# First stage of a three-block model: convolution taps moved from TensorE to ScalarE and GpSimd, level products summed before use, states in two PSUM banks

## The chip, the cores and the metric

The kernel runs on one core of a Trainium2 chip. The time is the device time of one execution in microseconds (us), and less is better. The engines are named as the profile names them: PE (TensorE), PEld (its weight loads), DVE (VectorE), ACT (ScalarE), POOL (GpSimd) and SP (SyncE, which only issues DMAs). SBUF is the on-chip working memory, PSUM the eight banks that PE writes its sums to.

## The reference, cut to what matters

A sequence of 256 tokens with 1024 features passes through a model of a first block with two layers and a second block. Each layer of the first block is a mixer and a product-key expert layer. Only the mixer of the first layer, `even_mix`, is touched:

```
p = h @ w_in                                  # h: rms-normed x
a_val, a_gate, q, k, v, r, glr = split(p)
# branch a, 512 channels: gate, causal depthwise convolution of 31 taps, layer norm, silu
u = a_val * sigmoid(a_gate)
y_a = silu(layer_norm(conv31(u) + conv_b))
# branch b, 4 heads of 64/128: gated linear attention in chunks of 64 tokens
log_a = log_sigmoid(glr @ gate_w2 + gate_b) / 16
attn[t,s] = sum_k q[t,k] k[s,k] exp(b[t,k] - b[s,k])   # b: cumulative log_a in the chunk, s <= t
o = (q exp(b)) @ state + attn @ v;  state = state*exp(b_last) + (k exp(b_last-b))^T @ v
y_b = rms_norm(o) * silu(r)
x = x + concat(y_a, y_b) @ w_out
```

The kernel computes the decayed attention of 128 tokens without dividing by small exponentials: it writes the causal triangle as seven "levels" (half widths 32, 16, 8, 4, 2, 1 and the diagonal). At each level the products of suitably scaled keys and queries are right on some blocks, which a 0/1 mask keeps; the sum over the levels is `attn`.

## The kernel before, in words

**Tiling.** Features lie on the 128 partitions, the 256 tokens on the free dimension. Weights arrive as a stream of blocks of 128x1024 in float32 (`Stream`, w_raw). ACT rounds each block to w_hi (L337), DVE subtracts for w_lo (L353), and a projection (`proj_t`) takes 24 PE passes: 8 slices of the features, each as hi*hi, hi*lo and lo*hi. A plain float32 product takes two PE passes instead. Blocks marked plain (row blocks 0 to 5) are used as float32 without the split.

**The first stage, in the order in which PE gets it** (`even`, L638): the values v (`natural`, 4 blocks), the small gate projection glr (`decays`), branch c=0 (aval, agate), keys and queries (kq, 4), branches c=1 to 3 (aval, agate), the output gates r (4), the rest of the eight chains, and the eight row blocks of w_out in the order 4, 5, 6, 7, 0, 1, 2, 3 (`Rows`). Row blocks 4 to 7 need the attention output (two heads each), 0 to 3 the convolution branch after its layer norm.

**What sets the order of the small work.** Every engine works through its instructions in program order, and the order is written by hand with two devices. `flow` is a list of generators: each call of `flow.step()` advances every one of them to its next `yield`. `bg` holds the convolution steps of DVE: `bg.run(slack)` issues steps until their nominal cost has used up the slack. `tick(n, slack)` (L900) adds the next chain if the levels are done, steps `flow` once and runs `bg`. There is one tick after each projection (slack 1200, three convolution steps), two after each r (2000, five steps each), one for each further chain, and one in each turn of the loop over the row blocks (2500). Evacuations of a projection are issued after the next projection (`lagged`, `flush`), those of r at once. The loop over the row blocks adds `layer_norm` when `bg` is empty, and a row block when its inputs are in the set `ready`.

**The convolution.** For each group c of 128 channels, `gated` writes ub, the gated input with 30 zero columns ahead. Taps 0 to 7 are done by PE (`conv_pe`, L775): POOL has made 8 diagonal matrices dg from the identity and the taps (`taps`, L656), and 8 float32 products, 16 passes, sum ub shifted by the tap into bank 7; ACT copies the sum to yp. Taps 8 to 30 are 23 steps on DVE into yc (`conv`, L765 and L769). `layer_norm` starts with yc += yp (L862), then mu_b, centring, squares, var, square root, rs_b, scaling and silu.

**The attention.** `decays` makes the scaled keys and queries z of the levels. `states` (L787) makes the three states, each in one PSUM bank taken from the list `pa`, which holds only bank 3 at this point. `inner` (L811) is a chain for one head and 128 tokens, eight in all. In its first tick it makes seven products pm, 14 passes, on 64 partitions, in banks 2 and 6; in the second DVE masks them into sm (L822, L823); in the third PE adds all seven sm times the values, and the states' share, into oT:

```
for l in range(7):
    mm(oT[p][...], vn[:, tb, hd * P:(hd + 1) * P], sm[:, l], p not in started, l == 6)
```

After chain 4 and chain 8 `head_norm` follows in three ticks: squares; o_ps and a square root; ob, two products and, for row blocks 6 and 7, a split (`parts`, which also marks the row blocks ready).

Of the kernel before, what the change touches and what calls it, by code (L numbers as in the profile page):

```python
# [20 lines left out]
P = 128  # L21
S = 256
# [19 lines left out]
EV_ROWS = (4, 5, 6, 7, 0, 1, 2, 3)  # L42
CONV_PE = 8
U_SLACK = 1300
# [334 lines left out]
def body(ctx: ExitStack, tc: tile.TileContext, a, out, phases=(0, 6)):  # L379
# [6 lines left out]
    class Banks:  # L386
# [5 lines left out]
        def set(self, banks):  # L392
            self.banks, self.i = banks, 0
# [16 lines left out]
    def acc(i, name="acc"):  # L410
        return psum.tile([P, 512], F32, tag=f"bank{4 + i}", name=f"{name}{i}")
# [15 lines left out]
    def col(name, i=0, n=1):  # L427
        at, w = COLS[name]
        assert i + n <= w
        return cols[:, at + i:at + i + n]  # L430
# [207 lines left out]
    def even():  # L638
        banks((0, 1), (2, 3))
        with even_pool as es:  # L640
# [7 lines left out]
            tri64, = masks(sp, 3, 4)  # L648
            dgs = deque()

            def taps():
                c = len(dgs) + pe_done
                if c < 4:
                    dg = tp.tile([P, CONV_PE, P], F32, name="dg", tag="dg")
                    for j in range(CONV_PE):
                        nc.gpsimd.tensor_scalar(dg[:, j], ident, col("convw", c * CONVW + j), None, op0=OP.mult)  # L656
                    dgs.append(dg)

            f2 = lambda t: t.rearrange("p a b -> p (a b)")
# [5 lines left out]
            def parts(k0, n):  # L665
                for k in range(k0, k0 + n):
                    if k in split_k:
                        i = split_k.index(k)
                        split_to(y[0][:, i], y[1][:, i], yf[:, k])
                    ready.add(k)  # L670

# [17 lines left out]
            def decays():  # L689
# [7 lines left out]
                proj_small(h, gws, ps[:16, :S], 16)  # L697
                while norm["steps"] is not None:
                    yield
# [64 lines left out]
            def conv(c):  # L764
                nc.vector.tensor_scalar(yc[:, c], ub[:, c, CONV_PE:CONV_PE + S], col("convw", c * CONVW + CONV_PE),  # L765
                                        col("convb", c), op0=OP.mult, op1=OP.add)
                yield 300
                for j in range(CONV_PE + 1, CONVW):
                    nc.vector.scalar_tensor_tensor(yc[:, c], ub[:, c, j:j + S], col("convw", c * CONVW + j),  # L769
                                                   yc[:, c], op0=OP.mult, op1=OP.add)  # L770
                    yield 400

            pe_done = 0

            def conv_pe(c):  # L775

                nonlocal pe_done
                pe = acc(3, "pe")
                dg = dgs.popleft()
                for j in range(CONV_PE):  # L780
                    mm(pe[:, :S], dg[:, j], ub[:, c, j:j + S], j == 0, j == CONV_PE - 1)
                yield
                nc.scalar.activation(yp[:, c], pe[:, :S], AF.Copy)
                pe_done += 1
                taps()

# [24 lines left out]
            def inner(hd, tb):  # L811
# [8 lines left out]
                yield  # L820
                sm = tp.tile([P, 7, P], F32, name="sm", tag="sm", bufs=2)
                nc.vector.tensor_mul(f2(sm[:, :4]), pm[0], f2(lmask[:, :4]))  # L822
                nc.vector.tensor_mul(f2(sm[:, 4:]), pm[1][:, :3 * P], f2(lmask[:, 4:]))  # L823
                yield
                if not oT:
                    oT.extend(psum.tile([P, 512], F32, tag=f"bank{i}", name="oT") for i in range(2))
                for l in range(7):
                    mm(oT[p][:, e * S + tb * P:e * S + (tb + 1) * P], vn[:, tb, hd * P:(hd + 1) * P], sm[:, l],
                       p not in started, l == 6)
                    started.add(p)  # L830
                for c in (2 * tb, 2 * tb + 1):
# [57 lines left out]

            ready = set()  # L890
            chains = deque(inner(2 * p + e, tb) for p in range(2) for tb in range(2) for e in range(2))
# [8 lines left out]
            def tick(n, slack):  # L900
                for _ in range(n):
                    if "levels" in done:
                        if "states" not in done:
                            done.add("states")
                            flow.add(states())
                        elif chains:
                            flow.add(chain(chains.popleft()))
                    flow.step()
                    bg.run(slack)
# [5 lines left out]
            for j in range(4):  # L915
                natural(va, j)
                if j == 1:
                    flow.add(decays())
                if j >= 2:
                    taps()  # L920
                flow.step()
# [7 lines left out]
            def branch(c):  # L929
# [7 lines left out]
                def gated():  # L937
# [5 lines left out]
                    bg.add(conv(c))  # L943
                    flow.add(conv_pe(c))

# [6 lines left out]
            for t, scale in ((kT, 1.0), (qT, 0.125)):  # L952
                for p in range(2):
# [3 lines left out]
                    tick(1, E_SLACK)  # L957
            banks((4, 5), (3,))
            flush()
# [13 lines left out]
            while len(chains) > E_LATE:  # L973
                tick(1, E_SLACK2)
            pm_banks[1] = 3
            rows = Rows(y, [split_k.index(k) if k in split_k else k for k in EV_ROWS], yf)
            while rows.n < 6:
# [870 lines left out]
```

## Time and profile before

| | us |
|---|---|
| time, median of 3 runs (lowest, highest) | 2348.55 (2344.61, 2349.74) |
| the profiled execution | 2352.38 |
| its span in the profile | 2350.6 |
| first row block of the stage begins (PE) | 138.41 |
| row block 0 begins (PE) | 161.52 |

Of the span PE is busy 99%, PEld 97%, DVE 73%, ACT 58% and POOL 4%. A busy PE isn't PE at its peak: its clock is granted at one of two levels, 1.2 and 2.4 GHz, and the column PEclk gives the mean of a stretch as a share of the upper one. "Busy" counts the time in which an engine has an instruction at work; a wait row names who ended an engine's idle time. The first stage ends, with the last row block, at about 175 us of the span; then the expert layer of the first layer begins, whose code isn't touched, nor is any later stage.

### The profile page before, as it was taken

How to read it: one execution, taken by the hardware profiler on the slowest of the kernel's cores; microseconds unless marked ns; L12 is line 12 of the kernel's file. 1: busy time of each engine (PE TensorE's matmuls, PEld its weight loads, DVE VectorE, ACT ScalarE, POOL GpSimd, SP SyncE). 2: the span in 40 equal slices, each digit the busy share in tenths (PEclk: the TensorE clock that was granted, in tenths of full speed). 3: DMA queues.
4: the chain of work that ended last, by engine and by line, in shares of the span. 5: the costliest groups of instructions: out<-in, count | busy, mean ns of one | idle time of the engine just before them, and what ended most of it. 6: DMA issues, size and time to landing. Idle time of an engine off the chain costs nothing. (4 is left out here: it accounts for less than half of the span.)

```text
span 2350.6 us, 48812 instructions
## 1 busy us (share of the span) xinstructions
PE 2315.8 (99%) x19664; PEld 2268.3 (97%) x19664; DVE 1723.3 (73%) x3656; ACT 1357.8 (58%) x2480; POOL 93.6 (4%) x107
## 2 busy tenths in 40 slices
PE   8999999999999999999999999999999999999999
PEld 7889999999999999998899999999999999999999
DVE  6668999999755555566699899996555555667983
ACT  6226448888544444455564588884444445555762
POOL 4100000000000000010000000000000000002300
PEclk9899999999999999999999999999999999999999
DMA  6114654444555666553256544446556565645553
GB/s 214 54 63 163 193 185 156 149 145 140 174 185 185 206 186 184 178 193 117 89 165 190 186 145 147 144 142 188 185 185 206 185 185 161 210 137 177 181 182 123
DMA packets 106626, 386.82 MB, mean 165 GB/s; under 512 B 11959, under 2 KB 13272, under 8 KB 106016
## 3 DMA queue, kind: packets, MB, share of 16 engines
q1 hardware_dynamic: 104976, 377.99, 50.7%
q0 software_dynamic: 1136, 5.32, 0.7%
q8 instruction: 154, 2.52, 0.4%
q14 instruction: 72, 0.59, 0.1%
q10 hardware_dynamic: 288, 0.40, 0.1%
HBM read 383.40 MB, written 1.05 MB: 164 GB/s over the span
## 5 line engine op out<-in xcount | busy, mean ns | idle before, releaser
L353 DVE TENSOR_TENSOR w_lo<-w_raw,w_hi 128x1024 fp32r<-128x1024 f32 x710 | 866.4, 1224 | 383.9 <-ACT w_hi L337 382.3
L337 ACT ACTIVATE w_hi<-w_raw 128x1024 fp32r<-128x1024 f32 x710 | 745.6, 1054 | 432.6 <-PE pv L452 348.0
L452 PE MATMUL pu<-h_hi,w_hi 128*128 128x256 f32 x2048 | 586.9, 287 | 0.0
L452 PE MATMUL pu<-h_lo,w_hi 128*128 128x256 f32 x2048 | 575.2, 281 | 0.0
L452 PE MATMUL pu<-h_hi,w_lo 128*128 128x256 f32 x2048 | 574.5, 281 | 0.0
L452 PE MATMUL pv<-h_hi,w_hi 128*128 128x256 f32 x1888 | 530.4, 281 | 0.0
L452 PE MATMUL pv<-h_lo,w_hi 128*128 128x256 f32 x1888 | 530.4, 281 | 0.0
L452 PE MATMUL pv<-h_hi,w_lo 128*128 128x256 f32 x1888 | 530.4, 281 | 0.0
L452 PEld LDWEIGHTS pu<-h_lo,w_hi 128*128 128x128 f32 x2048 | 386.4, 189 | 0.0
L452 PEld LDWEIGHTS pu<-h_hi,w_lo 128*128 128x128 f32 x2048 | 385.8, 188 | 0.0
L452 PEld LDWEIGHTS pu<-h_hi,w_hi 128*128 128x128 f32 x2048 | 385.5, 188 | 0.0
L452 PEld LDWEIGHTS pv<-h_hi,w_lo 128*128 128x128 f32 x1888 | 355.8, 188 | 0.0
L452 PEld LDWEIGHTS pv<-h_lo,w_hi 128*128 128x128 f32 x1888 | 355.8, 188 | 0.0
L452 PEld LDWEIGHTS pv<-h_hi,w_hi 128*128 128x128 f32 x1888 | 355.8, 188 | 0.0
L1271 ACT ACTIVATE X<-pu 128x256 f32<-128x256 f32 (+31 forms) x228 | 74.1, 325 | 197.2 <-PE pu L452 197.1
L1168 ACT ACTIVATE oa<-cb,routed 128x128 bf16<-128x128 f32 x512 | 162.9, 398 | 0.0
L1173 DVE TENSOR_TENSOR ob<-ob,g 128x512 bf16<-128x512 bf16 x256 | 108.0, 422 | 4.4
L452 PEld LDWEIGHTS <-oa 128*128 128x128 bf16 x1536 | 90.2, 96 | 12.9 <-issue 5.3
L452 PE MATMUL g<-ob,oa 128*128 128x128 bf16 x1024 | 102.1, 219 | 0.0
L452 PE MATMUL g<-oa 128*128 128x128 bf16 x512 | 94.7, 219 | 0.3
L461 DVE TENSOR_TENSOR h_lo<-X,h_hi 128x512 fp32r<-128x512 f32 (+1 forms) x134 | 86.4, 653 | 2.1 <-ACT h_hi L460 1.9
L1174 ACT ACTIVATE oa<-oa 128x512 bf16<-128x512 bf16 x128 | 80.8, 631 | 4.1
(450 smaller groups left out, 4122.3 us busy)
## 6 DMA issues: line engine op xcount, KB each, us to landing
w_raw<-in_s_u SPq DMA_DIRECT2D x256, 512.0 KB, 3.6
w_raw<-in_s_v SPq DMA_DIRECT2D x256, 512.0 KB, 3.6
w_raw<-in_s_mix SPq DMA_DIRECT2D x46, 512.0 KB, 3.9
w_raw<-in_s_up SPq DMA_DIRECT2D x44, 512.0 KB, 4.3
w_raw<-in_s_wq SPq DMA_DIRECT2D x32, 512.0 KB, 3.7
w_raw<-in_s_odd SPq DMA_DIRECT2D x32, 512.0 KB, 4.0
w_raw<-in_s_even SPq DMA_DIRECT2D x28, 512.0 KB, 3.9
w_raw<-in_s_down SPq DMA_DIRECT2D x22, 512.0 KB, 4.2
```

The source lines that it names most:

```text
L337: self.nc.scalar.activation(hi, raw, AF.Copy)
L353: self.nc.vector.tensor_sub(lo, raw, hi.bitcast(F32))
L452: nc.tensor.matmul(o, l, r, start=start, stop=stop, skip_group_check=True)
L461: nc.vector.tensor_sub(lo, src, hi.bitcast(F32))
L1168: nc.scalar.activation(o[0][:, i * P:(i + 1) * P], iota, AF.Abs, bias=ne1T[:, t0 + i:t0 + i + 1])
L1173: nc.vector.tensor_tensor(two[part], two[2], pairs(g3[:, part, t0:t0 + GT]), op=OP.mult)
L1174: nc.scalar.activation(o[0], o[0], AF.Relu, bias=1.0, scale=-1.0)
L1271: nc.scalar.activation(X(c)[:, td:], ps[:, td:S], AF.Gelu)
```

## The change

Five things are changed, all in `even`.

1. `conv_pe`, the diagonal matrices and their maker `taps` go. `conv_pool(c)` takes their place in `flow`: for each of taps 0 to 7 ACT writes ub shifted, times the tap, to a tile (tap 0 straight to yp, taps 1 to 7 to one of four tiles), and POOL adds the tile to yp. It does two taps per tick, so it takes four ticks for a group.
2. In `inner` POOL sums the seven masked levels in four adds (three levels to three, then 2 += 6, 0 += 1, 0 += 2), and PE then makes one float32 product with the values in place of seven. The chain has one more tick between masks and product, and sm has three buffers instead of two.
3. After kq the list `pa` holds banks 3 and 7 (bank 7 is free, as PE's convolution is gone) until the chains are all begun; then bank 3 alone.
4. `decays` begins after the first value block instead of the second, so that the split of the small gate weights and the glr products come one block earlier; it then waits until the sum of squares is complete.
5. `parts` marks row blocks in `late`, and `tick` moves them to `ready` at its start, so a row block is released one tick later.

The core of the diff:

```diff
-            dgs = deque()
-            def taps():
-                ...
-                    ready.add(k)
+                    late.add(k)
...
-                while norm["steps"] is not None:
+                while norm["steps"] is not None or norm["n"] < KD:
                     yield
...
-            def conv_pe(c):
-                pe = acc(3, "pe")
-                dg = dgs.popleft()
-                for j in range(CONV_PE):
-                    mm(pe[:, :S], dg[:, j], ub[:, c, j:j + S], j == 0, j == CONV_PE - 1)
-                yield
-                nc.scalar.activation(yp[:, c], pe[:, :S], AF.Copy)
-                ...
+            def conv_pool(c):
+                for j in range(CONV_POOL):
+                    t = tp.tile([P, S], F32, name="tap", tag="tap", bufs=4) if j else yp[:, c]
+                    nc.scalar.activation(t, ub[:, c, j:j + S], AF.Copy, scale=col("convw", c * CONVW + j))
+                    if j:
+                        nc.gpsimd.tensor_tensor(yp[:, c], yp[:, c], t, op=OP.add)
+                    if j % 2:
+                        yield
...
-                sm = tp.tile([P, 7, P], F32, name="sm", tag="sm", bufs=2)
+                sm = tp.tile([P, 7, P], F32, name="sm", tag="sm", bufs=3)
                 nc.vector.tensor_mul(f2(sm[:, :4]), pm[0], f2(lmask[:, :4]))
                 nc.vector.tensor_mul(f2(sm[:, 4:]), pm[1][:, :3 * P], f2(lmask[:, 4:]))
+                add = lambda o, a_, b_: nc.gpsimd.tensor_tensor(o, a_, b_, op=OP.add)
+                add(f2(sm[:, 0:3]), f2(sm[:, 0:3]), f2(sm[:, 3:6]))
+                add(sm[:, 2], sm[:, 2], sm[:, 6])
+                add(sm[:, 0], sm[:, 0], sm[:, 1])
+                add(sm[:, 0], sm[:, 0], sm[:, 2])
+                yield
                 yield
                 ...
-                for l in range(7):
-                    mm(oT[p][:, e * S + tb * P:e * S + (tb + 1) * P], vn[:, tb, hd * P:(hd + 1) * P], sm[:, l],
-                       p not in started, l == 6)
-                    started.add(p)
+                mm(oT[p][:, e * S + tb * P:e * S + (tb + 1) * P], vn[:, tb, hd * P:(hd + 1) * P], sm[:, 0],
+                   p not in started, True)
+                started.add(p)
...
+                    ready.update(late)
                     flow.step()
                     bg.run(slack)
...
-                if j == 1:
+                if j == 0:
                     flow.add(decays())
-                if j >= 2:
-                    taps()
...
-                    flow.add(conv_pe(c))
+                    flow.add(conv_pool(c))
...
-            banks((4, 5), (3,))
+            banks((4, 5), (3, 7))
...
             pm_banks[1] = 3
+            banks((4, 5), (3,))
```

## Rows read from the trace of the kernel before

**Rows 1.** the page: busy time, share of the span and count of each engine

```profile
PE 2315.8 (99%) x19664; PEld 2268.3 (97%) x19664; DVE 1723.3 (73%) x3656; ACT 1357.8 (58%) x2480; POOL 93.6 (4%) x107
```

**Rows 2.** windows: stretch, length, busy PE, PEld, DVE, ACT, POOL, PEclk, DMA, GB/s

```profile
32.00:84.00 52.00, 47.35 (x331) 44.43 (x332) 44.93 (x84) 27.56 (x44) 15.88 (x19) 0.97 0.37 121
84.00:122.00 38.00, 36.20 (x230) 33.74 (x229) 19.79 (x48) 3.53 (x6) 0.00 (x0) 0.78 0.05 14
122.00:162.00 40.00, 35.66 (x263) 33.28 (x263) 27.75 (x59) 8.23 (x17) 0.00 (x0) 1.00 0.16 53
```

**Rows 3.** waits of PE, first 200 us: total, times, longest

```profile
PE pe L452 <- DVE ub L942: 3.4, 2, 2.5
...
PE glr L452 <- DVE gws_l L461: 1.2, 1, 1.2
...
PE s_ps L452 <- DVE state L802: 1.1, 1, 1.1
...
PE s_ps L452 <- DVE state L800: 0.7, 1, 0.7
```

**Rows 4.** timeline of PE: start, length, operation, count; one convolution group

```profile
74.38 3.62 PE L452 MATMUL pe<-ub,dg 128*128 128x256 f32 x16
```

**Rows 5.** timeline of PE: sm products, pm and r

```profile
99.59 3.35 PE L452 MATMUL oT<-sm,vn 128*128 128x128 f32 x14
...
103.19 2.93 PE L452 MATMUL pm<-z 64*128 64x128 f32 x12
...
106.47 0.58 PE L452 MATMUL r<-h_hi,w_hi 128*128 128x256 f32 x1
...
111.71 1.73 PE L452 MATMUL oT<-sm,vn 128*128 128x128 f32 x14
...
113.53 1.60 PE L452 MATMUL pm<-z 64*128 64x128 f32 x12
...
115.29 1.83 PE L452 MATMUL oT<-sm,vn 128*128 128x128 f32 x14
```

**Rows 6.** windows, instructions of tile r alone

```profile
119.20:122.17 2.97, 2.97 (x24) 2.92 (x24) 0.00 (x0) 1.00 0.00 0
```

**Rows 7.** windows of 4 us, PEclk third from the end

```profile
64.00:68.00 4.00, 4.00 (x13) 3.23 (x12) 4.00 (x10) 0.27 (x1) 0.00 (x0) 0.59 0.42 135
88.00:92.00 4.00, 3.57 (x29) 3.31 (x30) 2.26 (x7) 0.00 (x0) 0.00 (x0) 0.89 0.00 0
```

**Rows 8.** waits of DVE, 36 to 84 us

```profile
DVE ub L942 <- ACT sg L941: 4.6, 4, 3.1
DVE qT L955 <- PE kq L452: 0.9, 1, 0.9
```

**Rows 9.** timeline of DVE, then POOL, 173 to 175 us

```profile
173.25 0.48 DVE L486 SCALAR_TENSOR_TENSOR h_lo<-xT,cols,h_hi 128x256 fp32r<-128x256 f32 x1
...
174.25 1.02 DVE L486 SCALAR_TENSOR_TENSOR h_lo<-xT,cols,h_hi 128x256 fp32r<-128x256 f32 x1
...
174.26 0.73 POOL L494 TENSOR_TENSOR sqacc<-sqacc,z 128x256 f32<-128x256 f32 x1 [97.53 <-ACT z L492]
```

**Rows 10.** timeline of DVE: mask products and five convolution steps

```profile
96.28 0.68 DVE L822 TENSOR_TENSOR sm<-pm,lmask 128x512 f32<-128x512 f32 x1
96.88 0.55 DVE L823 TENSOR_TENSOR sm<-pm,lmask 128x384 f32<-128x384 f32 x1
97.35 2.06 DVE L769 SCALAR_TENSOR_TENSOR yc<-ub,cols,yc 128x256 f32<-128x256 f32 x5
```

**Rows 11.** groups of ACT by form, 0 to 180 us: a scaled copy

```profile
L483 ACT ACTIVATE h_hi<-xT,cols 128x256 fp32r<-128x256 f32 x16 | 7.5, 502 | 7.1 <-DVE xT L504 6.5 <-DMA xT<-in_xT 0.7
```

**Rows 12.** timeline of PE: layer norm and row block 0

```profile
150.66 1.99 PE L452 MATMUL mu_b<-yc,cb 128*128 128x256 f32 x8 [1.06 <-DVE sr L853]
...
155.35 1.84 PE L452 MATMUL var_ps<-cb,csq 128*128 128x1 f32 x16
...
161.52 0.48 PE L452 MATMUL rows<-yf,w_raw 128*128 128x256 f32 x1 [1.15 <-ACT yf L884]
```

More of the change, by code (lines that the diff above doesn't have):

```diff
@@ L42 @@
 EV_ROWS = (4, 5, 6, 7, 0, 1, 2, 3)
-CONV_PE = 8
+CONV_POOL = 8
 U_SLACK = 1300
@@ L648, in even @@
             tri64, = masks(sp, 3, 4)
-            dgs = deque()
-            def taps():
-                c = len(dgs) + pe_done
-                if c < 4:
-                    dg = tp.tile([P, CONV_PE, P], F32, name="dg", tag="dg")
-                    for j in range(CONV_PE):
-                        nc.gpsimd.tensor_scalar(dg[:, j], ident, col("convw", c * CONVW + j), None, op0=OP.mult)
-                    dgs.append(dg)
             f2 = lambda t: t.rearrange("p a b -> p (a b)")
@@ L764, in conv @@
             def conv(c):
-                nc.vector.tensor_scalar(yc[:, c], ub[:, c, CONV_PE:CONV_PE + S], col("convw", c * CONVW + CONV_PE),
+                nc.vector.tensor_scalar(yc[:, c], ub[:, c, CONV_POOL:CONV_POOL + S], col("convw", c * CONVW + CONV_POOL),
                                         col("convb", c), op0=OP.mult, op1=OP.add)
                 yield 300
-                for j in range(CONV_PE + 1, CONVW):
+                for j in range(CONV_POOL + 1, CONVW):
                     nc.vector.scalar_tensor_tensor(yc[:, c], ub[:, c, j:j + S], col("convw", c * CONVW + j),
@@ L771, in conv @@
                     yield 400
-            pe_done = 0
-            def conv_pe(c):
-                nonlocal pe_done
-                pe = acc(3, "pe")
-                dg = dgs.popleft()
-                for j in range(CONV_PE):
-                    mm(pe[:, :S], dg[:, j], ub[:, c, j:j + S], j == 0, j == CONV_PE - 1)
-                yield
-                nc.scalar.activation(yp[:, c], pe[:, :S], AF.Copy)
-                pe_done += 1
-                taps()
+            def conv_pool(c):
[6 more added lines that the diff above has]
+                        yield
             def states():
@@ L888, in layer_norm @@
                 yield
-            ready = set()
+            ready, late = set(), set()
             chains = deque(inner(2 * p + e, tb) for p in range(2) for tb in range(2) for e in range(2))
@@ L916, in even @@
                 natural(va, j)
-                if j == 1:
+                if j == 0:
                     flow.add(decays())
-                if j >= 2:
-                    taps()
                 flow.step()
```

## The prediction

> **What bounds the kernel now.** First the busy table of the page [rows 1]: the reader sees PE busy for 99% of the span, so time is won only where PE waits, runs slowly or does work that can go. Next the busy time by stretch [rows 2], since the change touches only the first stage, which ends with the last row blocks at about 175 us; everything after it starts when it ends and needs no word. Three stretches differ. From 32 to 84 us PE is busy 47.4 of 52 us, but DVE 44.9 too, and DVE waits for PE little [rows 8]: the two are level. From 84 to 122 us PE is busy 36.2 of 38 us at a mean granted clock of 0.78, while DVE is busy for half. From 122 to 162 us PE is at full clock with 4.3 us of gaps, and DVE is busy for two thirds. Then PE's waits [rows 3], the lengths of the products that go [rows 4, 5], and the clock [rows 7].
>
> The clock needs care. The same 14 passes of sm products and their state passes take 3.60 us from 99.59 and 1.82 us from 111.71; pm takes 3.28 us from 103.19 and 1.76 us from 113.53; r takes 5.24 us from 106.47 and 2.97 us from 119.20 [rows 5, 6]. So PE ran at 1.2 GHz there, and at 2.4 GHz after. The clock fell after PE had been idle for 2.5 us waiting for ub [rows 3, 7], and again between 88 and 92 us [rows 7], after states and pm, which use 64 rows of the array, with a wait between. It held from 112 us on, where every pm was followed by as long a run of 128-row sm products [rows 5].
>
> **The change part by part.**
>
> *Convolution taps off PE.* Four groups of 16 passes go, 3.6 us each [rows 4], 14 us, and with them the 3.4 us of waits for ub [rows 3]. But three groups lie before 84 us, where DVE sets the pace: its own queue is unchanged, and only the waits of DVE for PE can go: 0.9 us [rows 8] and three smaller ones, some 1.5 us; its waits for ACT stay. In their place come 32 scaled copies on ACT, 0.50 us each by the nearest scaled copy [rows 11], 16 us; ACT is busy 27.6 of 52 us and 3.5 of 38 [rows 2], so they are covered, and without cover cost at most 2 of them per tick, 1 us. On POOL, 28 adds of 128x256 take 0.73 us each [rows 9], 20 us, instead of 32 diagonal scalings.
>
> The adds are not free for DVE. The same STT (two SBUF sources, like a convolution step) takes 0.48 us alone and 1.02 us when an add on POOL started 10 ns after it, +0.54 [rows 9]. Bounds for one add: 0 if it falls beside an evacuation from PSUM, 0.54 if it meets such a step. 17 adds lie before 84 us, so 0 to 9.2 us; I take 2.5, as POOL waits too and the old scalings already cost something. Stretch one: -1.5 + 2.5 = +1.0.
>
> *The seven levels summed before the product.* Of 14 passes, 12 go from each of 8 chains. 16 passes take 1.82 us [rows 5], so 12 x 0.114 = 1.4 us, 11 us in all. POOL gets four adds per chain of 384 and 3 x 128 columns, by area three times 0.73, 2.2 us; 8 chains 17.5 us. DVE does the same two mask products. The sum comes two ticks before its use, and a tick holds at least 3.1 us of DVE work (1.1 us of masks issued back to back and 2.06 us of five convolution steps [rows 10]), so one sum is covered; behind the 11 adds of the last two convolution groups the first may be late by up to 3 us, and then pm and r, queued on PE behind that oT, wait too. With only 0.4 us of oT per tick PE can no longer hide DVE: pm needs the banks that the mask products read.
>
> *States in two banks.* Removes waits of 1.1 and 0.7 us [rows 3]; late next is the mask product that frees pm's bank, so part of this comes back.
>
> *Early gate projection.* Its weights' low half no longer stands behind the sums of squares: 1.2 us of wait [rows 3] becomes about 0.4, -0.8 us. This lies on PE's path before 32 us, and the start of everything after moves with it.
>
> *One more tick for a chain, and rows released one tick later.* Both delay nothing that PE lacks work for until the rows. There, before, row blocks 6 and 7 stood between the steps of the layer norm: mu_b at 150.66, var at 155.35, row block 0 at 161.52 [rows 12]. After the change the second head norm ends two ticks later, so those two blocks stand behind the layer norm's products, and nothing covers its steps; o_ps and mu_b also share bank 3 in turn.
>
> **Stretch two, from the end of r0 (83.7) to the end of r3 (122.3), 38.6 us now.** What is left for PE at full clock: three r (9), five pm (9), three states (2), oT (1), 21 us; it waits for DVE and DVE for r. One after the other: a first round of 6.2 (two states, pm, r), one of 10.1 (r, masks, ten convolution steps, states, pm), one of 9.0, together 25.3; with 23 add equivalents at 0.54 that meet DVE's two-source work about half the time, +6.2, 31.5. That is -7.1. At half clock the PE work alone is 3 x 5.2 + 5 x 3.3 + 3.5 + 1.5 = 37.1, hiding DVE: -1.5. Which one? After the change a tick of this stretch holds pm on 64 rows and waits, and no long run of 128-row products: what stood before the fall near 91 us, not what stood in 112 to 122 us. I take half clock, -1.5; bounds -7.1 and +3 (POOL late).
>
> **Stretch three, end of r3 to row block 0, 39.2 us now.** At full clock, one step after another: three ticks of pm and masks to 11, seven convolution steps, two norm products of 512 columns and block 4 to 19.7, block 5 to 23.2, mu_b 24.9; then the uncovered steps (centring, o_ps, square root, var, square root, ob, two products, split) 8.3 us from the small rows of their kind, 33.2; blocks 6 and 7 to 39.2. So 0, or +2 with the port shared. At half clock: each pm tick 4.2 instead of 3.1 (+3.5), block 4 by its nearest row, r, +2.3, blocks 6 and 7 after a stretch of small products +2.3: about +9 with +1 for the port. I take +9; bounds 0 and +14.
>
> **Sum.** -0.8 + 1.0 - 1.5 + 9 = +7.7 us. The profiled execution took 2352.38 us (span 2350.6), 3.8 above the median of the runs, 2348.55; against its own time the sum gives 2360, against the median 2356.
>
> A rule of the Trainium skill speaks against the change (SBUF — State Buffer, section "Who interferes with whom"): a VectorE instruction with two SBUF inputs and a GpSimd instruction that reads SBUF exclude each other, each for its whole length. The trace agrees in kind; its +0.54 of a 0.73 us add is less than the whole [rows 9]. By the rule the sum is the third rival below.
>
> **The rivals.**
>
> 1. *The clock holds, not slower.* Place: 84 to 122 us. It decides if the r projections, dense and of 128 rows, keep the clock at 2.4 GHz between the pm. For it: r at half clock ended with the clock back up at 111.7 [rows 5]; against: the fall near 91 us with less waiting than the change leaves. Sum: -0.8 + 1.0 - 7.1 + 1 = -5.9, 2343 us.
> 2. *The clock falls but recovers in r3*, so stretch three is at full clock: -0.8 + 1.0 - 1.5 + 2 = +0.7, 2349 us. For it: r2 did so before [rows 5]. Against: PE then meets 8 us of small norm products with nothing between.
> 3. *POOL's port becomes the bound.* If each add shuts DVE out for its whole 0.73 us, 38 us of POOL work stand in DVE's queue. From 32 to 150 us DVE is busy some 84 us now [rows 2]; with 38 and its waits of 4.6 for ACT [rows 8] that is 127 in a stretch of 118, +9, and +6 for what the forecast's clock still adds behind it: about +15, 2363 us. For it: rows 9; against: evacuations and mask products read PSUM and need no second source.
>
> That the taps on ACT and POOL come too late for the layer norm speaks from no row: they end some 35 us ahead of it.
>
> **How the numbers follow.** Forecast 0.50, rivals 0.15, 0.22 and 0.13. Below 0.2% (4.7 us) a measurement of this kernel tells nothing from no change: 2343.9 to 2353.2. Faster: most of rival 1 and a little of 2, 0.17. Same: most of rival 2 and the low end of the forecast, 0.25. Slower: 0.58. The forecast's own range is 2351 to 2361; the one for 8 in 10 reaches to rivals 1 and 3, 2342 to 2365.
>
> **What would show it.** Granted clock near 0.5 in most of the stretch from r1 to row block 4, and again before block 6, shows the clock step right; near 1 throughout shows rival 1. Convolution steps in pairs stretched beside POOL's adds, with DVE's busy time up by over 20 us, show rival 3. PE waiting for POOL's sums ahead of oT shows the backlog. PE's gaps between mu_b and block 6 of over 4 us show the lost cover. The end of r3 later than 125 us makes stretch two wrong, and a stage that ends before 170 us the whole forecast.

## The result and the profile after

The changed kernel takes **2366.79 us** (median of 4 runs, 2365.04 to 2368.61); the kernel before took 2348.82 us beside it (2344.61 to 2349.74). The ratio is 1.008 (95% interval 1.0063 to 1.0098): 18.0 us slower. The forecast was 2356 us with a range of 2342 to 2365: the sign was right, the size was not. Most of what was missed lies in the first stretch of the stage, where 7.2 us were lost and 1.0 was foreseen. The profiled execution of the changed kernel took 2365.04 us (span 2363.2).

The busy line of the page, changed kernel; it answers to [rows 1]:

```profile
PE 2307.1 (98%) x19504; PEld 2259.6 (96%) x19504; DVE 1740.1 (74%) x3656; ACT 1369.9 (58%) x2508; POOL 110.8 (5%) x135
```

PE has 160 instructions fewer and is busy 8.7 us less. DVE has the same 3656 instructions and is busy 16.8 us more. That is the whole case in one line: work left PE, and the same DVE work became longer.

The windows of the changed kernel over the stretches of [rows 2]:

```profile
32.00:84.00 52.00, 36.88 (x255) 35.26 (x253) 44.67 (x73) 31.48 (x57) 15.54 (x17) 0.86 0.34 103
84.00:122.00 38.00, 29.02 (x181) 27.17 (x182) 33.11 (x57) 9.75 (x19) 19.83 (x27) 0.72 0.10 28
122.00:162.00 40.00, 33.49 (x163) 30.31 (x162) 27.72 (x51) 4.83 (x10) 10.61 (x16) 0.71 0.16 53
```

In the first, DVE is as busy as before (44.67 against 44.93 us) but gets 73 instructions done in place of 84. In the second it is busy 33 of 38 us. PE is far from busy in both, and its clock is 0.86 and 0.72.

PE's waits in the first 200 us of the changed kernel (total, times, longest), against [rows 3]:

```profile
PE pm L452 <- DVE sm L808: 10.6, 6, 3.4
...
PE aval L452 <- DVE va_sb L923: 5.3, 2, 3.9
PE r L452 <- DVE va_sb L923: 5.1, 1, 5.1
PE z_ps L452 <- issue: 3.7, 1, 3.7
```

The waits for ub, the gate weights and the states are gone. In their place PE waits for DVE's mask products (pm's banks) and for the evacuations va_sb, which stand in DVE's queue behind stretched steps. PE has no wait of oT for POOL's sums. Not all of these waits come from stretching: part of them appears as soon as PE has less work, as the experiment with fills shows.

What stretched them, DVE and then POOL of the changed kernel at 76 to 80 us (start, length):

```profile
76.80 0.42 DVE L734 TENSOR_TENSOR z<-z,kT 128x256 f32<-128x256 f32 x1
77.14 0.97 DVE L735 TENSOR_TENSOR z<-z,qT 128x256 f32<-128x256 f32 x1
78.03 0.96 DVE L734 TENSOR_TENSOR z<-z,kT 128x256 f32<-128x256 f32 x1
78.91 0.96 DVE L735 TENSOR_TENSOR z<-z,qT 128x256 f32<-128x256 f32 x1
...
76.78 2.81 POOL L769 TENSOR_TENSOR yp<-yp,tap 128x256 f32<-128x256 f32 x3 [7.67 <-ACT tap L767]
```

The same product takes 0.42 us when it starts together with POOL's first add (0.02 us after it; that add took 1.04 us) and 0.96 beside the next ones, +0.54 each. Five convolution steps beside adds took 4.04 us (here the row, with POOL's below); [rows 10] had 2.06:

```profile
93.61 4.04 DVE L759 SCALAR_TENSOR_TENSOR yc<-ub,cols,yc 128x256 f32<-128x256 f32 x5
...
91.35 6.02 POOL L769 TENSOR_TENSOR yp<-yp,tap 128x256 f32<-128x256 f32 x7 [7.44 <-ACT tap L767]
```

**By stretch.** The table is read from PE's timelines; each column is a difference of two starts or ends. Start: the product n_rb of the small gate projection. One: from there to the end of r0. Two: to the end of r3. Three: to the start of row block 0. End: the start of the first product behind the stage. The last column is the median less that of the kernel before measured beside it; that one lay between 2346.62 and 2348.82, so a difference of two entries is good to about 2 us. The stretches are those of one execution each, and that execution lies up to 3.6 us from its kernel's median; the first two rows, one kernel, are 6.2 us apart in stretch two and 1.6 in three, so smaller differences there show no cause by themselves. The experiments are told below.

| kernel | start | one | two | three | end | time |
|---|---|---|---|---|---|---|
| before, profiled execution | 31.29 | 52.4 | 38.6 | 39.2 | 175.25 | |
| before, profiled again | 31.36 | 52.4 | 32.4 | 40.8 | 170.67 | |
| after | 30.25 | 59.6 | 35.1 | 50.0 | 188.60 | +18.0 |
| taps only | 30.34 | 59.6 | 31.5 | 43.5 | 178.63 | +7.1 |
| sum only | 30.19 | 52.4 | 41.2 | 50.3 | 187.70 | +18.4 |
| after, no adds | 30.23 | 53.5 | 29.4 | 46.1 | 172.87 | +2.9 |
| after, no lateness | 30.16 | 58.8 | 36.6 | 42.9 | 182.18 | +10.8 |
| after, fills for adds | 30.26 | 49.7 | 28.7 | 48.6 | 170.88 | +1.3 |
| after, filler products | 30.19 | 58.5 | 37.5 | 47.1 | 186.89 | +15.7 |
| before, lateness | 31.89 | 52.4 | 35.1 | 44.3 | 177.31 | +7.6 |
| before, gate and banks | 30.42 | 52.4 | 31.7 | 40.8 | 169.04 | -2.0 |
| after, no tap adds | 30.32 | 53.6 | 35.2 | 50.5 | 183.16 | +9.8 |
| after, no level adds | 30.10 | 59.3 | 34.5 | 46.1 | 183.59 | +12.7 |
| after, no adds, no lateness | 30.26 | 52.6 | 31.1 | 41.2 | 168.83 | -3.5 |

Row blocks 0 to 3 take 13.6 to 13.7 us in all of them. From start to end the changed kernel lost 17.9 us against the second execution of before (-1.1 + 7.2 + 2.7 + 9.2 - 0.1 in the last row blocks) and 13.4 against the first: the forecast was built on an execution that was late by itself, which the last experiment shows.

### The profile page after: what moved, and what is told of

The parts are those of the page before. It is cut to its first block, busy times and chain, and to the rows that moved or that the text cites. A ratio compares the mean times of both kernels' runs of the same rounds, so it can differ in the third digit from the quotient of the medians.

```text
span 2363.2 us, 48572 instructions
## 1 busy us (share of the span) xinstructions
PE 2307.1 (98%) x19504; PEld 2259.6 (96%) x19504; DVE 1740.1 (74%) x3656; ACT 1369.9 (58%) x2508; POOL 110.8 (5%) x135
## 5 line engine op out<-in xcount | busy, mean ns | idle before, releaser
L452 PEld LDWEIGHTS <-oa 128*128 128x128 bf16 x1536 | 90.2, 96 | 12.8 <-issue 5.1
```

The source lines that it names most:

```text
L452: nc.tensor.matmul(o, l, r, start=start, stop=stop, skip_group_check=True)
```

## The experiments

Three theories stood against each other after the result. **Port:** POOL's adds read SBUF and stretch DVE's two-source instructions; DVE sets the pace, so PE waits. **Clock:** with the dense products gone PE drops to 1.2 GHz, and that is the price. **Cover:** the later release leaves the layer norm's steps uncovered.

**Taps alone.** The changed kernel with the seven level products back on PE and without the extra tick; rows are still released late.

```diff
-                add(f2(sm[:, 0:3]), f2(sm[:, 0:3]), f2(sm[:, 3:6]))
-                ...
-                yield
-                mm(oT[p][...], vn[...], sm[:, 0], p not in started, True)
+                for l in range(7):
+                    mm(oT[p][...], vn[...], sm[:, l], p not in started, l == 6)
```

> The changed kernel, but each chain again makes seven products with the masked levels on PE, with no adds on POOL and no extra tick (the order of before); the 28 tap adds on POOL stay. Port theory (DVE's steps with two SBUF sources wait for POOL's adds): r0 still ends 5 to 6 us later than before (89 to 90 us), the 11 tap adds behind it cost 3 to 4 more, the rest is as before: 2350 to 2356 us. Clock theory (the half clock follows from the missing 128-row products): PE is back at 2.4 GHz from r2 on, and the time falls to that of before or below, 2343 to 2349 us. Cover theory (row blocks 6 and 7 come too late): little changes against the changed kernel, 2360 to 2366 us.

Measured: 2353.74 us against 2346.62, ratio 1.0027 (1.0016 to 1.0037). The time lies in the band of the port theory. Stretch one is as long as in the whole change (59.6), stretches two and three are not. So the loss of stretch one, 7.2 us, belongs to the taps.

**The sum alone.** The kernel before with the level sum on POOL, the extra tick, the late release and the early gate projection; the taps stay on PE, the states in one bank.

```diff
+                add(f2(sm[:, 0:3]), f2(sm[:, 0:3]), f2(sm[:, 3:6]))
+                ...
+                yield
-                for l in range(7):
-                    mm(oT[p][...], vn[...], sm[:, l], p not in started, l == 6)
+                mm(oT[p][...], vn[...], sm[:, 0], p not in started, True)
...
-                    ready.add(k)
+                    late.add(k)
...
-                if j == 1:
+                if j == 0:
                     flow.add(decays())
```

> The kernel before with the sum of the seven levels on POOL, the extra tick, the late release and the early gate projection; the first eight taps stay on PE. Port theory: no loss before r0 (its end at 82 to 84 us), then five convolution steps beside each sum take 3.4 us instead of 2.1 us: 8 x 1.3 = 10 us of DVE, half of it hidden: 2352 to 2357 us. Clock theory: half clock from states to row block 4 as in the changed kernel, 2358 to 2366 us. Cover theory: some 10 us in the layer norm's stretch, 2356 to 2360 us.

Measured: 2365.06, ratio 1.0079 (1.0062 to 1.0095). Stretch one is as before (52.4), two is the longest of all, and three is as long as in the whole change. The time lies in the band of the clock theory and 8 us above that of the port theory: r1, r2 and r3 took 5.5, 4.9 and 5.0 us, and the clock from 84 to 122 us was 0.70. With +7.1 for the taps and +18.4 for this, the parts don't add up to +18.0: with the sum in place it hardly mattered any more whether PE also made the convolution's products. Why is not shown; this run doesn't part adds, lateness and half clock from each other.

**No adds.** The changed kernel without POOL's 28 + 32 adds; both sums are left out of the computation.

```diff
-                    if j:
-                        nc.gpsimd.tensor_tensor(yp[:, c], yp[:, c], t, op=OP.add)
-                add(f2(sm[:, 0:3]), f2(sm[:, 0:3]), f2(sm[:, 3:6]))
-                ...
```

> The changed kernel without any of POOL's adds: 28 tap adds and 32 level adds are left out, so yp holds tap 0 alone and the product uses level 0 alone; ACT's copies, the ticks and PE's work stay as in the changed kernel. Port theory: DVE's steps return to 0.48 us and five of them to 2.1 us, DVE's busy time in the stage falls by 12 to 16 us, and the time by 10 to 14: 2352 to 2357 us. Clock theory: PE's work is as thin as before, DVE less late lets PE wait less, but r, pm and row block 4 stay at half clock for most of the stretch: 2358 to 2364 us. Cover theory: 2360 to 2366 us.

Measured: 2349.53, ratio 1.0009 (1.0 to 1.0019), 2.5 us under the lower end of the port theory, the nearest of the three. Without the adds nearly all of the loss is gone, although lateness is still there, and half clock in part: from 84 to 122 us the clock is 0.86 in place of 0.72, from 122 to 162 us 0.70 in place of 0.71.

**No lateness.** The changed kernel without the extra tick and with rows released at once.

```diff
-                yield
                 yield
                 if not oT:
-                    late.add(k)
+                    ready.add(k)
```

> The changed kernel with the release of the row blocks as before (at once) and with no extra tick between masks and product; all adds stay. Cover theory: row blocks 6 and 7 stand between the layer norm's steps again, the stretch from r3 to row block 0 falls from 49 to 41 us: 2356 to 2360 us. Port and clock theories: at most 3 us come back and PE waits longer for POOL's sums ahead of oT, 2363 to 2370 us.

Measured: 2357.4, ratio 1.0045 (1.0028 to 1.0062), as the cover theory had it. Stretch three falls from 50.0 to 42.9 us. Two PE rows of this kernel, beside the same two of the changed kernel behind them, show how:

```profile
157.59 0.48 PE L452 MATMUL mu_b<-yc,cb 128*128 128x256 f32 x1 [1.06 <-DVE sr L844]
...
159.23 0.47 PE L452 MATMUL rows<-y_hi,w_hi 128*128 128x256 f32 x1
```

```profile
155.69 0.38 PE L452 MATMUL mu_b<-yc,cb 128*128 128x256 f32 x1
...
159.19 0.35 PE L452 MATMUL o_ps<-cb,osq 128*128 128x1 f32 x2 [1.60 <-ACT csq L862]
...
165.87 0.47 PE L469 MATMUL rs_b<-cb,cst 128*128 128x128 f32 x1 [0.78 <-DVE sr L845]
...
167.10 0.58 PE L452 MATMUL rows<-y_hi,w_hi 128*128 128x256 f32 x1 [0.55 <-ACT y_hi L460]
```

From mu_b to row block 6 it is 1.6 us in the one and 11.4 in the other.

**Fills in place of adds.** This parts the port from a mere wait for a slow POOL: each add becomes a fill of zeros of about the same length, at the same place in the queues, and both sums are left out.

```diff
-                    t = tp.tile([P, S], F32, name="tap", tag="tap", bufs=4) if j else yp[:, c]
+                    tw = tp.tile([P, 2 * S], F32, name="tap", tag="tap", bufs=4)
+                    t = tw[:, :S] if j else yp[:, c]
...
-                        nc.gpsimd.tensor_tensor(yp[:, c], yp[:, c], t, op=OP.add)
+                        for _ in range(2):
+                            nc.gpsimd.memset(tw[:, :450], 0.0)
...
-                sm = tp.tile([P, 7, P], F32, name="sm", tag="sm", bufs=3)
+                sm = tp.tile([P, 8, P], F32, name="sm", tag="sm", bufs=3)
...
-                add(f2(sm[:, 0:3]), f2(sm[:, 0:3]), f2(sm[:, 3:6]))
-                ...
+                for _ in range(3):
+                    nc.gpsimd.memset(f2(sm), 0.0)
```

> The changed kernel, with every add on GpSimd replaced by a fill of zeros that takes about as long (two fills of 450 columns for a tap's add, three of 1024 columns for the sum of a head's levels); the sums are left out. GpSimd stays as busy, it is waited for at the same places, but reads nothing. Port theory (an add that reads SBUF slows VectorE's two-source instructions): a fill doesn't, so convolution steps fall back from a mean of 649 to below 520 ns, VectorE's busy time from 1740 to about 1722 us, and the time to that of the kernel without adds, 2350 +/- 4. Latency theory (the price is PE waiting for a late GpSimd): steps may fall, the time stays at 2360 or above. A theory that any SBUF traffic of GpSimd slows VectorE: steps stay at 649 ns, 2366.

Measured: 2348.74 us against 2347.41, ratio 1.0 (0.9989 to 1.0011). The busy line of its page, then its convolution steps and fills from the groups by form (busy, mean ns of one), then the step group of the changed kernel:

```profile
PE 2298.6 (98%) x19504; PEld 2251.7 (96%) x19504; DVE 1721.6 (73%) x3656; ACT 1369.3 (58%) x2508; POOL 113.3 (5%) x155
...
L759 DVE SCALAR_TENSOR_TENSOR yc<-ub,cols,yc 128x256 f32<-128x256 f32 x88 | 39.4, 481 | 1.2
...
L771 POOL MEMSET tap<- 128x450 f32 x56 | 25.8, 480 | 48.0 <-ACT tap L768 46.2
L814 POOL MEMSET sm<- 128x1024 f32 x24 | 22.9, 952 | 8.5 <-DVE sm L811 7.3
```

```profile
L759 DVE SCALAR_TENSOR_TENSOR yc<-ub,cols,yc 128x256 f32<-128x256 f32 x88 | 54.4, 649 | 1.2
```

POOL is busier than with the adds (113.3 against 110.8 us), and DVE is 18.5 us less busy; a step takes 481 ns in place of 649. Where the z products took 0.96 us beside adds, they take 0.42 beside fills:

```profile
72.54 0.42 DVE L735 TENSOR_TENSOR z<-z,qT 128x256 f32<-128x256 f32 x1
72.88 0.43 DVE L734 TENSOR_TENSOR z<-z,kT 128x256 f32<-128x256 f32 x1
...
72.11 7.02 POOL L771 MEMSET tap<- 128x450 f32 x14 [5.63 <-ACT tap L768]
```

PE's waits for DVE are shorter, but not gone:

```profile
PE pm L452 <- DVE sm L810: 5.5, 6, 1.7
...
PE r L452 <- DVE va_sb L922: 3.4, 1, 3.4
PE aval L452 <- DVE va_sb L922: 3.2, 2, 2.4
```

Against 10.6, 5.1 and 5.3 us with adds, a third to a half of these waits comes from the adds; the rest stays when DVE is no longer slowed.

So it is what POOL reads that costs, not that it works or is waited for. The Trainium skill says the same (SBUF — State Buffer, section "Who interferes with whom"): a VectorE instruction with two SBUF inputs contends with a GpSimd instruction that reads SBUF and not with one that only writes it. The runs agree, with 0.42 against 0.96 us.

The windows of this kernel also answer the clock theory:

```profile
84.00:122.00 38.00, 32.50 (x197) 30.22 (x196) 28.97 (x65) 8.49 (x15) 29.08 (x41) 0.74 0.01 3
122.00:162.00 40.00, 34.33 (x162) 30.44 (x163) 19.00 (x37) 10.46 (x20) 2.13 (x3) 0.73 0.24 80
```

The mean granted clock is as low as in the changed kernel (0.72 and 0.71), and yet the time is that of the kernel before. Half clock alone thus does not make the loss; with the work that left PE, it is about paid for.

**Filler products.** Six more 128-row products per chain, whose sum is never used, with the states back in one bank.

```diff
+                junk = acc(3, "junk")
+                for l in range(1, 7):
+                    mm(junk[:, :P], vn[...], sm[:, l], l == 1, l == 6)
                 mm(oT[p][...], vn[...], sm[:, 0], p not in started, True)
-            banks((4, 5), (3, 7))
+            banks((4, 5), (3,))
```

> The changed kernel with six more 128-row products of a level's size per chain, into bank 7, whose sum is never used (the states go back to one bank for it). Clock theory (TensorE falls to 1.2 GHz because the dense products are gone, and the price is the half clock): the clock of 84 to 162 us rises from 0.72 to over 0.9, and the time falls by 3 to 9 us although TensorE does 11 us more work at full clock, 2357 to 2363. Port and cover theory (VectorE, slowed by GpSimd's adds, sets the pace, and the half clock is mostly slack): the time stays within 3 us of 2366, whatever the clock does. If TensorE's own work sets the pace, it is slower, 2370 to 2378.

Measured: 2363.11, ratio 1.0061 (1.004 to 1.0081). That is at the slow end of the clock theory's band (2363) and at the fast end of the port and cover theory's (2366 less 3), so the time by itself decides nothing. Its second and third window:

```profile
84.00:122.00 38.00, 30.07 (x190) 28.16 (x191) 28.69 (x51) 9.74 (x19) 17.20 (x24) 0.73 0.09 28
122.00:162.00 40.00, 35.91 (x257) 33.57 (x255) 32.44 (x56) 4.83 (x10) 13.48 (x20) 0.96 0.16 53
```

The clock came back in the third stretch (0.96 in place of 0.71) but not in the second. Stretch three is 2.9 us shorter, with PE doing more work there. So half clock may have a price of about that size in stretch three (one execution each), and 0.73 with the dense products back shows that their lack isn't all that lowers it in stretch two: PE is busy 30 of 38 us there and still waits.

**Lateness on the kernel before.** Only the extra tick (three buffers for sm) and the late release.

```diff
+                yield
                 yield
                 if not oT:
-                    ready.add(k)
+                    late.add(k)
```

> The kernel before with the extra tick of a chain (three buffers for sm) and the release of row blocks one tick later, nothing else: all level products stay on TensorE. Cover theory (with the second head norm two ticks later, row blocks 6 and 7 stand behind the layer norm and its steps are uncovered): 5 to 10 us slower than before, 2352 to 2357, and gaps of over 4 us between mu_b and row block 6. Rival (the lost cover costs only when TensorE has no dense products left and VectorE is slowed): within 3 us of before, 2347 +/- 3.

Measured: 2355.03 against 2347.41, ratio 1.0026 (1.0013 to 1.004). Stretch three 44.3 against 40.8 and 39.2, and from the end of mu_b to row block 6 it is 8.4 us, as the cover theory had it. Lost cover thus costs where PE's work is as before, too: 3.5 to 5.1 us in the stretch, 7.6 in the median. By the last column it costs 7.2 us on the changed kernel (18.0 less 10.8) and 6.4 without adds (2.9 less -3.5): nearly the same in all three. How much of this is idle time and how much a lower clock isn't parted: the ten executions run from 2349.57 us at a mean clock of 0.996 to 2360.47 at 0.991, and the two at 0.995 took 2350.13 and 2350.58, where the kernel before took 2350.71 and 2351.61 in its two at 0.995.

**Gate projection and banks on the kernel before.**

```diff
-                if j == 1:
+                if j == 0:
                     flow.add(decays())
-            banks((4, 5), (3,))
+            banks((4, 5), (3, 7))
...
             pm_banks[1] = 3
+            banks((4, 5), (3,))
```

> The kernel before with only two of the five edits: the gate projection one value block earlier, and two banks (3 and 7) in turn for the states (and what follows them up to the end of the chains). If these two parts are gains as the prediction has it, 1 to 3 us faster than before, 2344 to 2346; if bank 7, which TensorE's convolution also takes in this kernel, gives a new wait, 0 to 3 us slower.

Measured: 2345.37 against 2347.41, ratio 0.9986 (0.9976 to 0.9995). The start is 0.9 us earlier, as the prediction had it. Its window from 84 to 122 us has the clock at 0.96:

```profile
84.00:122.00 38.00, 36.39 (x290) 34.02 (x289) 26.15 (x63) 5.41 (x8) 0.00 (x0) 0.96 0.04 13
```

It is the fastest kernel here that computes all of the reference, by 2.0 us; the interval lies wholly below 1, but the gain is smaller than the 0.2% named in the prediction.

**Each kind of add by itself.** The changed kernel without the tap adds, and without the level adds (the sum in question is left out).

```diff
-                    if j:
-                        nc.gpsimd.tensor_tensor(yp[:, c], yp[:, c], t, op=OP.add)
```

> The changed kernel without the 28 adds of the taps on GpSimd (their sum is left out; ScalarE still makes the scaled copies); the level sums stay. Port theory: stretch one loses its 6 us (r0 ends near 84 instead of 89.9 us), and the time falls by 6 to 10 us, 2356 to 2360. If the adds only matter where a chain waits for a sum, the tap adds cost nothing, and the time stays at 2363 to 2367.

```diff
-                add(f2(sm[:, 0:3]), f2(sm[:, 0:3]), f2(sm[:, 3:6]))
-                ...
```

> The changed kernel without the 32 adds that sum a head's levels (the product uses one level alone; the rest of the sum is left out); the tap adds stay. Port theory: stretch one stays as in the changed kernel (r0 ends near 90 us), and the stretches behind it lose 5 to 10 us: 2356 to 2361. If the price lies wholly in the tap adds, 2364 to 2367.

Measured: 2357.15, ratio 1.004 (1.0028 to 1.0052), and 2359.98, ratio 1.0046 (1.0025 to 1.0067). By the last column the tap adds cost 8.2 us, 6.0 of them in stretch one (53.6 in place of 59.6), and the level adds 5.3, of which 3.9 in stretch three. Together 13.5, against 15.1 for both at once (and 16.7 by the fills): the parts nearly add up. Stretch two is an exception. Neither alone shortens it (35.2 and 34.5 against 35.1), both together do (29.4). In these executions r2 and r3 took 5.5 and 5.4 us without the tap adds and 5.3 and 4.2 without the level adds, against 4.1 and 4.5 in the changed kernel; so the clock was another in each, and what each kind of add costs in stretch two stays open.

**No adds, no lateness.** What is left is the work taken off PE.

```diff
-                        nc.gpsimd.tensor_tensor(yp[:, c], yp[:, c], t, op=OP.add)
-                add(f2(sm[:, 0:3]), f2(sm[:, 0:3]), f2(sm[:, 3:6]))
-                ...
-                yield
-                    late.add(k)
+                    ready.add(k)
```

> The changed kernel with no adds on GpSimd at all (both sums left out) and without the extra tick and the late release: what is left is the work taken off TensorE. If port and cover are the two prices and they add up (17 and 9 us), 2366 - 26 = 2340, 7 us faster than before: the gain that the change had in it. If the half clock is a third price of its own, the time stays at 2345 to 2350.

Measured: 2343.78 against 2347.32, ratio 0.9981 (0.997 to 0.9991). So with nothing put in their place but ACT's copies, 25 us of PE work (14 and 11 by the prediction) were worth 3.5 us, 1.1 of it from the gate projection. The three stretches, 52.6, 31.1 and 41.2, are about those of the kernel before (52.4, 32.4, 40.8). The second window of this kernel shows why:

```profile
84.00:122.00 38.00, 34.07 (x206) 31.87 (x205) 26.42 (x63) 9.46 (x19) 0.00 (x0) 0.74 0.05 14
```

PE is busy for 34 of 38 us with 206 records in place of the 281 that the second execution of before has there, at a clock of 0.74 in place of 0.96: what it saved in work it spent at half clock. The result lies between the two sums expected: half clock is a price of its own, but one that comes out of PE's savings.

**The kernel before, profiled again.**

> The kernel before, unchanged, profiled a second time. The execution behind the prediction had a mean granted clock of 0.994 and took 2352.38 us; other executions of the same kernel have 0.996 to 0.998 and 2344 to 2349 us. If the stretch from 84 to 122 us, at a clock of 0.78 in that execution, is what differs, an execution near the median shows over 0.9 there, r1 and r2 take about 3.1 us each instead of 4.6 and 5.4, and the last row block ends at 170 to 172 us instead of 175. If the stage looks as it did, the spread lies in a later stage.

Measured: 2347.77 us, granted clock 0.996. The windows of 4 us of PE (busy, PEclk), this execution and then the one behind the prediction:

```profile
92.00:96.00 4.00, 3.46 (x21) 0.72 0.00 0
96.00:100.00 4.00, 3.42 (x31) 1.00 0.00 0
100.00:104.00 4.00, 4.00 (x34) 1.00 0.01 4
104.00:108.00 4.00, 4.00 (x36) 1.00 0.00 0
```

```profile
92.00:96.00 4.00, 3.39 (x19) 0.68 0.00 0
96.00:100.00 4.00, 3.49 (x24) 0.75 0.00 0
100.00:104.00 4.00, 4.00 (x20) 0.50 0.00 0
104.00:108.00 4.00, 4.00 (x19) 0.50 0.02 4
```

In both the clock falls at the same place, in r1 behind the states and pm, and r1 takes 4.6 us in both, not the 3.1 expected. In one it is back at 96 us and r2 takes 3.10 us; in the other it falls again and stays down until 111 us, and r2 takes 5.4. The stage ends 4.58 us apart (170.67 and 175.25), and the executions differ by 4.61.

## Why the prediction was right and wrong

**The step that failed** is the port's term, "I take 2.5" for stretch one (bounds 0 to 9.2): it measured 6.0. The same term was then taken in stretch two as something that half clock hides. Stretch one came out at +7.2 instead of +1.0. With the adds left out it is 53.5 and 53.6, so the adds are 6.0 of it, where 2.5 stood, and the rest +1.2, where -1.5 stood. That relief of PE was there, but half clock took it: with fills, at a clock of 0.97, the stretch is 49.7, -2.7 (and the adds by that comparison 9.9); without adds, at 0.87, r0 took 5.45 us after a wait of 3.3, in place of 3.07 after the same wait. The first of its 24 passes without adds, then with fills:

```profile
78.29 0.55 PE L452 MATMUL r<-h_hi,w_hi 128*128 128x256 f32 x1 [3.35 <-DVE va_sb L916]
```

```profile
76.85 0.36 PE L452 MATMUL r<-h_hi,w_hi 128*128 128x256 f32 x1 [3.35 <-DVE va_sb L922]
```

The value was chosen because POOL waits too, the old scalings already cost something, and an add beside an evacuation costs nothing. The rows say otherwise: most of DVE's queue beside the adds, z products and convolution steps, reads two tiles of SBUF, and lengthens by about what [rows 9] showed: 0.54 us for a z product, 0.40 for a convolution step (4.04 us for five against 2.06). The old scalings were worth little: DVE was busy 1723.3 us with them and 1721.6 with fills. The row was there; it was discounted without a row for the discount.

**Stretch two** was forecast at -1.5 for the profiled execution and came out at -3.5, which looks right and is luck. The reason given was that PE at half clock hides DVE. The clock did fall, but not throughout: r1, r2 and r3 took 3.10, 4.13 and 4.47 us, where the sum had 5.2 for each. The fills leave the clock at 0.74 and the stretch at 28.7 us, and the kernel without adds has 29.4: in the 35.1 us of the changed kernel DVE was busy for 33 of 38, slowed by the adds, and PE waited for it, so most likely DVE set the pace; the experiments with one kind of add left out do not confirm it. That r3 ended at 125.02 us, past the 125 set as the sign of a wrong stretch two, comes from the loss in stretch one. Full work at full clock was given as 25.3 us, 31.5 with the port; 35.1 was measured at a clock of 0.72.

**The base.** Forecast and measurement were compared with a median, but the sum was made on an execution 3.8 us above it. The prediction carried the sum over from the one to the other as it was. That holds if the extra time lies where the change does not touch it; it lay in stretch two, r2 at half clock, which the change rewrites. Against an execution near the median stretch two is +2.7, not -3.5. 12.7 us separate the two profiled executions (7.7 forecast), 18.0 the medians. Of the 10.5 us by which the forecast missed, 5.0 are thus the sum's own. Of the rest, 3.6 to 3.8 are the base, and 1.8 are that the profiled execution of the changed kernel lay below its median.

**Stretch three** was forecast at +9 and came out at +10.8 (+9.2 against the second execution). That is near, but the split was another, so the number is in part luck. In the sum half clock made 8 of the 9, the port 1, and the uncovered steps no loss at full clock (its 39.2 is the time before). Measured, lateness is the largest part, 7.1 (42.9 without); the steps between mu_b and row block 6, put at 8.3 us, took 9.5 from the end of mu_b (157.58). The port has 1.4 to 3.9 us in it (48.6 with fills, 46.1 without level adds), and half clock some 2.9 by the filler products. These overlap and do not sum.

**The start** was right: -0.8 forecast, -1.0 in the profile.

**The rivals.** The first (clock holds) fell: 0.72 in stretch two. The second, too: the clock did not recover in r3, which took 4.5 us. The third, POOL's port as the bound, had a chance of 0.13 and came nearest: the mechanism was its own, though an add cost DVE 0.40 to 0.54 us, not its whole length. Its sign was DVE's busy time up by over 20 us with steps stretched in pairs; it rose by 16.8, and the steps from a mean of 484 to 649 ns. Its 2363 was still 4 us short. It counted 0.73 us for an add; a tap's add took 0.874 on average, and POOL's adds 46 us together (24.3, 12.8 and 9.0 by its groups) in place of 38.

**What would have shown it** beforehand: counting, in DVE's queue from 32 to 150 us, the instructions with two sources in SBUF and giving each add 0.54 us of them. For stretch one that is the upper bound of 9.2 us that the prediction itself gave, and it lies between the 6.0 and the 9.9 measured. The 32 to 84 us window already had the two engines level, so such a loss was likely to lie on the path.

## What to carry to other kernels

Before work moves to GpSimd, look at what VectorE does beside it: where that has two SBUF sources and its engine sets the pace, an add of 128x256 on GpSimd costs up to 0.54 us of VectorE, and the 60 adds cost this kernel 15 to 17 us, while fills of the same length cost nothing that shows (2348.74 us against 2349.53 with neither). Work taken off an engine that then waits for another, or runs at half clock, buys little (25 us of TensorE work, 3.5 us of time), and can take away the cover of a chain of small steps. Profile the kernel before twice, or hold the profiled execution's granted clock beside those of the timed runs, before a forecast rests on a stretch whose clock was low.

## What the runs showed of the hardware beyond this

One program's executions spread with the granted clock: of 25 executions of the kernel before, the fastest took 2343.79 us at a mean clock of 0.998 and the slowest 2354.91 at 0.993, with the others nearly in order between. The two profiles show one place where it comes from: the same fall of the clock near 92 us ends at 96 us or at 111 us. What decides between the two is open; the instructions up to there have the same times to 0.1 us.

The slowing of VectorE by an add is less than the add's whole length. Seven convolution steps, 0.41 us each alone by the five in [rows 10], stood beside seven adds that took 6.02 us, and took 1.83 + 4.04 = 5.87: one step per add, each pair 0.86 us, less than the 1.14 us that a step and an add of 0.73 would take one after the other. The two steps ahead of the five shown above:

```profile
91.46 1.83 DVE L759 SCALAR_TENSOR_TENSOR yc<-ub,cols,yc 128x256 f32<-128x256 f32 x2
```

Nor is it always VectorE that pays. Two of the w_lo (two sources in SBUF, 128x1024, 1.22 us in the kernel before) met an add. The one that began 0.46 us into an add took 1.41 us, the add 0.79. The one that began 0.17 us ahead of an add took 1.23, the add 1.66 in place of some 0.73:

```profile
39.38 1.41 DVE L353 TENSOR_TENSOR w_lo<-w_raw,w_hi 128x1024 fp32r<-128x1024 f32 x1
...
48.75 1.23 DVE L353 TENSOR_TENSOR w_lo<-w_raw,w_hi 128x1024 fp32r<-128x1024 f32 x1
...
48.92 1.66 POOL L769 TENSOR_TENSOR yp<-yp,tap 128x256 f32<-128x256 f32 x1
```

In these two the later one paid. The start alone does not settle it: the product at 76.80 us, begun 0.02 us after an add, was not slowed, and the one in [rows 9], begun 0.01 us ahead, was. So a count of two-source instructions gives a bound of what adds cost VectorE, not the cost.

The mask products, which read PSUM and one tile of SBUF, took 0.68 and 0.54 us beside adds in the changed kernel (103.62 and 104.22 us), as in [rows 10]: they are not slowed.
